# Seven products in place of eight for the first half of the gate's projection, in both layers of a hybrid trunk

## The chip, the cores and the metric

The kernel runs on one core of one Trainium2 chip. The metric is the device time of one execution in microseconds (us), the median of the runs shown. Engines are named as in the profile: PE is TensorE (matmuls), PEld its weight loads, DVE is VectorE, ACT is ScalarE, POOL is GpSimd, SP issues the loads.

## The reference

256 tokens, width 2048, two layers, everything in float32. Cut to what matters here:

```
h = rms_norm(x, norm1_g[l])
q, k, v, gu, gv = split(h @ w_in[l])           # 1024 columns each
attn = dilated_attention(rotary(q), rotary(k), v)        # 8 heads of 128
v2   = layer_norm(gelu(gv)) per group of 128 columns     # gv is "the gate"
gm   = gelu(gu) * (tril(w_spatial) @ v2 + b_spatial)     # 8 groups of 128
x = x + concat(attn, gm) @ w_out[l]
x = x + square(relu(rms_norm(x, norm2_g[l]) @ w_up[l])) @ w_down[l]
out = rms_norm(x, final_g)
```

## The kernel before, in words

Each float32 matmul is made of three in a reduced format: weight and activation are split into a high and a low part, and high·high, low·high and high·low are added in PSUM. The activations `x` lie transposed in SBUF; `hs` holds the two parts of `x` times the norm's gain (the norm's factor itself is multiplied in later).

**Pieces and steps.** The weights come in pieces of 128 x 1024 numbers (`Sub`, L145). SP loads a piece into one of 7 buffers `raw`, ACT copies it into the high part `hi` (L168), DVE subtracts to get the low part `lo` (L178); there are 6 buffers of each, so the sixth piece ahead has to wait until TensorE has left the first. One step of the program uses one piece. There are three kinds:

- a *plain* step (`transposed`, L376): 24 matmuls with 256 columns (L410), the weight is the stationary operand, the result comes out transposed. q and k are made so, in 8 groups of four steps: k0 (256 columns of k), q0, k1, q1, ... q3. After a group come the rotary positions (`after_qk`, L572: two copies on ACT, L577 and L578, then three operations on DVE, L579 to L581);
- a *natural* step (`natural`, L454): 12 matmuls with 512 columns (L470 to L472), 8 steps for 512 columns. v and the gate are made so, in two halves each;
- a *seven-product* step (`fast`, L414), which before is used in the MLP's second matrix alone: Strassen's scheme in Winograd's form on a 2 x 2 block. It has 42 matmuls with 256 columns (L440) and counts as four pieces: `Top` and `Bottom` are loaded, `Sums` twice are made of them by DVE (two subtractions of 128 x 512 each, L219 and L220, L223 and L224), and each of the four needs its `hi` and `lo` (of `Top` half the width). Two such steps make one block of 1024 rows. It also needs sums of the activations, made beforehand by four DVE operations (L803 to L806) and split by `to_half` (L644).

**The order.** Every engine takes its instructions in the order in which the program writes them. The main loop (L1007) goes through the list of steps. For step n it writes, in this order: `hi` of pieces up to five after the step's own (`high_to`; for a `Sums` piece its subtractions as well), what is due (`soon`), `lo` of pieces up to four after (`low_to`), loads, the step's matmuls, what follows a finished group, hooks, and then entries of a queue (`later`) whose delay, counted in pieces, is over. Entries of the list without a piece (`mark`) also let the queue run. So a piece's `lo` is written four pieces ahead, and whatever else DVE and ACT have to do is written between.

**A layer's first half.** v (natural, 16 steps), then k0, q0, k1, q1, ... q3 (32 plain steps), then the gate (natural, 16 steps), the other gate operand gu (plain, 16 steps) and the output matrix. The attention of a pair of heads is put in the queue when its q group ends: `scores` 2 pieces later (TensorE L593, L596; DVE L602, L604), `normalise`, `turn` (transposes), `values`. The gate's halves pass through `gelu`, statistics (`stats`, DVE) and `layer_norm` (POOL).

Of the kernel before, what the change touches and what calls it, by code (L numbers as in the profile page):

```python
# [28 lines left out]
F32 = mybir.dt.float32  # L29
# [38 lines left out]
HALVES = 5  # L68
BEHIND, BETWEEN = 2, 1
D_SCORES, D_NORM, D_TURN, D_VALUES = 2, 1, 3, 2  # L70

# [20 lines left out]
def trunk(ctx: ExitStack, tc: tile.TileContext, layout, xT, consts, gains, w, b_sp, w_sp, out):  # L92
# [8 lines left out]
    pacc = ctx.enter_context(tc.tile_pool(name="pacc", bufs=1, space=bass.MemoryType.PSUM))  # L101
    paux = ctx.enter_context(tc.tile_pool(name="paux", bufs=4, space=bass.MemoryType.PSUM))

# [31 lines left out]
    def acc_bank(i=None, of=4):  # L135
# [277 lines left out]

    def fast(name, l, row0, col0, tiles, slots, fresh, last, done):  # L414

# [5 lines left out]
        for p in range(2):  # L421
# [3 lines left out]
            def mm(p=p, top=top, bottom=bottom, upper=upper, lower=lower):  # L425
                if p == 0:
                    o.extend(slots())
                half = tiles[0][0]
                sums_ready()
                extra = sum_parts[0]  # L430
                left, right = slice(0, 256), slice(256, 512)
# [43 lines left out]
    def mark(fn):  # L475

        steps.append((None, fn, None))

    def from_hs(k):
# [38 lines left out]
    def layer(l, n1, n2, n3, last):  # L518
# [27 lines left out]
        if l:  # L546
            mark(start)
        mix_a, mix_g = [None], [None]
        qk = {}
# [107 lines left out]
        def after_gv(c, ps):  # L657
            z, u = t32("gz", [2, 512], tag="tmpB"), t32("gu", [2, 512], tag="tmpA")
            for tt in range(2):
                act.activation(z[:, tt, :], ps[tt], AF.Copy, scale=n1.half[:, tt:tt + 1])  # L660

            def then(u, z):
# [5 lines left out]
                later(1, 1.5, lambda: stats(c // P))  # L668

            gelu(z, u, then)  # L670

        def stats(g0):
# [8 lines left out]
            later(0, 1.0, lambda: layer_norm(g0))  # L681

        def layer_norm(g0):
            y, mv = par["y"], par["mv"]
            r = t32("lr", [2, 4])
            rsqrt(nc.gpsimd, r, mv[:, :, g0:g0 + 4, 1], 1.0, LN_EPS, [2, 4])
            for g in range(4):
                for tt in range(2):
                    yg = y[:, tt, (g0 + g) * P:(g0 + g + 1) * P]
                    nc.gpsimd.tensor_scalar(yg, yg, mv[:, tt, g0 + g, 0:1], r[:, tt, g:g + 1],  # L690
                                            op0=OP.subtract, op1=OP.mult)
            par["normed"] += 4
# [107 lines left out]
        def sums():  # L800

            a11, a12, a21, a22 = (inner[:, 4 * k:4 * k + 4, t * P:(t + 1) * P] for t in range(2) for k in range(2))
            vec.tensor_tensor(a22, a21, a22, op=OP.add)  # L803
            vec.tensor_tensor(a21, a11, a21, op=OP.subtract)
            vec.tensor_tensor(a11, a22, a11, op=OP.subtract)
            vec.tensor_tensor(a12, a12, a11, op=OP.subtract)  # L806

# [33 lines left out]
        def turn_back(c, first, second, bank):  # L841
# [5 lines left out]
            soon(1, lambda: update(n3, c, ps, False, last))  # L847

        def halves(bank):
            return [bank[:, 0:256], bank[:, 256:512]]  # L850

# [61 lines left out]
        for e in range(9):  # L913
# [5 lines left out]
            if e:  # L919
                w = 512 * len(ORDER.get(e, USUAL))  # L920
                hidden = [hid[e - 1]]
                down = collect(transposed, "w_down", l, (e - 1) * 1024, 8, w, D - w, from_tiles(hidden, NH),
                               lambda c, ps, e=e, w=w: after_down(e, (c + w) // P, ps),
                               apart=last and e == 8, of=2 if e < 8 else 4,
                               cols=None if e < 8 else [c * P for c in LAST])
                for g, at in enumerate(ORDER.get(e, USUAL)):
                    banks = []
                    quick += zip(at, collect(fast, "w_down", l, (e - 1) * 1024, 512 * g, hidden,
                                             (lambda g=g, banks=banks: slots_other(g, banks)) if g else slots_first,
# [146 lines left out]
```

## Time and profile before

| what | before |
|---|---|
| device time, median of 3 runs | 2023.7 us (2023.22 to 2024.14) |
| time of the profiled execution | 2023.7 us, of it 2021.9 us span |
| busy share of the span: PE, DVE, ACT, POOL | 99%, 78%, 60%, 8% |
| granted TensorE clock, mean | 0.997 |
| instructions | 40716, of them 16810 matmuls |

The span is the time from the first to the last instruction on the chip; 1.8 us of the execution lie around it. A line such as L410 is a line of the kernel before.

### The profile page before, as it was taken

Reading aid. Unit: us, or ns where it says so; the run is one execution under the profiler, and the core shown is the slowest. Engines: PE = TensorE matmul, PEld = TensorE weight load, DVE = VectorE, ACT = ScalarE, POOL = GpSimd, SP = SyncE. Lnnn points to the kernel's source line nnn. Section 1 sums busy time; section 2 is a strip of 40 time slices with the busy share of each in tenths; the row PEclk is TensorE's granted clock in tenths of the full one; section 3 lists DMA queues with packets and bytes.
Section 4 is the critical chain, followed back from the end, with each engine's and each line's share of the span. In section 5 each row is a group of like instructions: output and inputs, shape, how many; then the busy total and the mean of one; then the engine's idle time right before and its main releaser. Section 6 shows DMA issues by size and latency. Waiting matters only on the chain.

```text
span 2021.9 us, 40716 instructions
## 1 busy us (share of the span) xinstructions
PE 2009.5 (99%) x16810; PEld 1973.4 (98%) x16810; DVE 1579.8 (78%) x1954; ACT 1221.2 (60%) x1613; POOL 156.2 (8%) x200
## 2 busy tenths in 40 slices
PE   9999999999999999999999999999999999999997
PEld 8998999999999999999989989999999999999997
DVE  7566766688888898898856667667888898888985
ACT  7565455566566666665645654556666666667653
POOL 0002300000001000100000032000000000010000
PEclk9999999999999999999999999999999999999998
DMA  9555556566678776866664555565676776777662
GB/s 330 192 167 167 187 189 202 174 229 204 222 219 239 240 225 203 249 215 215 201 215 158 168 187 188 188 199 179 217 229 208 228 236 216 239 220 241 212 215 81
DMA packets 126442, 419.26 MB, mean 207 GB/s; under 512 B 14128, under 2 KB 22064, under 8 KB 126256
## 3 DMA queue, kind: packets, MB, share of 16 engines
q1 hardware_dynamic: 110800, 389.86, 57.2%
q0 software_dynamic: 14304, 23.86, 6.5%
q8 instruction: 131, 2.15, 0.4%
q10 hardware_dynamic: 1152, 2.94, 0.4%
q14 instruction: 55, 0.45, 0.1%
HBM read 394.58 MB, written 22.02 MB: 206 GB/s over the span
## 4 chain that ended last, share of the span: by engine, by line
PE 99%; DVE 0%; ACT 0%; issue 0%; DVEq 0%
PE acc L410 70%; PE acc L440 10%; PE aux L440 8%; PE acc L470 3%; PE acc L472 3%; PE acc L471 3%; PE aux L699 0%; PE aux L635 0%; PE aux L593 0%; PE aux L622 0%; PE aux L994 0%; DVE x L1038 0%; PE aux L596 0%; PE aux L637 0%; PE acc L846 0%; PE aux L539 0%
## 5 line engine op out<-in xcount | busy, mean ns | idle before, releaser
L168 ACT ACTIVATE hi<-raw 128x1024 fp32r<-128x1024 f32 (+1 forms) x817 | 836.9, 1050 | 487.5 <-DVE raw L220 216.2
L178 DVE TENSOR_TENSOR lo<-raw,hi 128x1024 fp32r<-128x1024 f32 (+1 forms) x817 | 965.3, 1214 | 143.4 <-ACT hi L168 140.4
L410 PE MATMUL acc<-hs,hi 128*128 128x256 f32 x5632 | 985.9, 277 | 0.0
L410 PEld LDWEIGHTS acc<-hs,hi 128*128 128x128 f32 x5632 | 857.9, 188 | 0.4 <-issue 0.2
L410 PE MATMUL acc<-hs,lo 128*128 128x256 f32 x2816 | 778.0, 276 | 0.0
L410 PEld LDWEIGHTS acc<-hs,lo 128*128 128x128 f32 x2816 | 528.7, 188 | 0.4 <-issue 0.2
L410 PE MATMUL acc<-half,hi 128*128 128x256 f32 x2688 | 462.2, 276 | 0.0
L410 PEld LDWEIGHTS acc<-half,hi 128*128 128x128 f32 x2688 | 406.7, 188 | 0.0
L410 PE MATMUL acc<-half,lo 128*128 128x256 f32 x1344 | 371.0, 276 | 0.0
L410 PEld LDWEIGHTS acc<-half,lo 128*128 128x128 f32 x1344 | 252.3, 188 | 0.0
L873 POOL DMA_DIRECT2D far<-ar x92 | 74.2, 816 | 1164.4 <-ACT ar L876 563.9
L440 PE MATMUL acc<-hi,shared 128*128 128x256 f32 x768 | 138.4, 276 | 0.0
L440 PEld LDWEIGHTS acc<-hi,shared 128*128 128x128 f32 x768 | 119.2, 188 | 0.0
L440 PE MATMUL aux<-hi,half 128*128 128x256 f32 x528 | 110.6, 276 | 0.0
L440 PE MATMUL acc<-lo,shared 128*128 128x256 f32 x384 | 106.0, 276 | 0.0
L649 DVE TENSOR_TENSOR half<-ar,half 128x512 fp32r<-128x512 f32 x72 | 49.8, 691 | 68.6 <-ACT half L646 68.6
L470 PE MATMUL acc<-hi,hs 128*128 128x512 f32 x256 | 101.8, 398 | 0.0
L472 PE MATMUL acc<-hi,hs 128*128 128x512 f32 x256 | 100.6, 393 | 0.0
L471 PE MATMUL acc<-lo,hs 128*128 128x512 f32 x256 | 100.3, 392 | 0.0
L440 PEld LDWEIGHTS aux<-hi,half 128*128 128x128 f32 x528 | 87.2, 188 | 0.0
L440 PE MATMUL aux<-hi,shared 128*128 128x256 f32 x448 | 80.7, 276 | 0.0
L510 DVE TENSOR_TENSOR x<-x,acc 128x512 f32<-128x512 f32 (+1 forms) x49 | 33.1, 675 | 59.1 <-PE acc L410 57.3
(150 smaller groups left out, 1955.3 us busy)
## 6 DMA issues: line engine op xcount, KB each, us to landing
raw<-in_w SPq DMA_DIRECT2D x731, 512.0 KB, 4.7
far<-ar POOLq DMA_DIRECT2D x60, 256.0 KB, 8.3
far<-ar POOLq DMA_DIRECT2D x32, 128.0 KB, 4.3
ar<-far POOLq DMA_DIRECT2D x12, 256.0 KB, 9.7
raw<-in_w SPq DMA_DIRECT2D x10, 256.0 KB, 5.1
x<-in_xT SPq DMA_DIRECT2D x7, 256.0 KB, 5.9
out<-x SPq DMA_DIRECT2D x7, 256.0 KB, 3.1
shared<-in_b_sp ACTq DMA_DIRECT2D x2, 512.0 KB, 7.7
```

The lines of the kernel that those rows point to most:

```text
L168: act.activation(self.h[:, j * m:(j + 1) * m], self.raw[:, j * m:(j + 1) * m], AF.Copy)
L178: vec.tensor_tensor(lo[:, r], self.raw[:, r], self.h[:, r].bitcast(F32), op=OP.subtract)
L410: pe.matmul(o, lhsT=lhs, rhs=xs[:, rhs, :], start=(first and j == 0), stop=(last and j == 2), skip_group_check=True)
L440: calls.append(lambda k=k, j=j, lhs=lhs, rhs=rhs: pe.matmul(o[n], lhsT=lhs, rhs=rhs, start=(p == 0 and k == 0 and j == 0 and n in fresh), ...
L470: pe.matmul(ps, lhsT=xh, rhs=hi, start=(k0 + k == 0), stop=False)
L471: pe.matmul(ps, lhsT=xh, rhs=lo, start=False, stop=False)
L472: pe.matmul(ps, lhsT=xl, rhs=hi, start=False, stop=(k0 + k == KC - 1))
L510: vec.tensor_tensor(xj, xj, ps[j][:, 0:S] if alone else pair(ps)[:, j, :], op=OP.add)
L649: vec.tensor_tensor(t[:, c:c + 2, 1, :], src, t[:, c:c + 2, 0, :].bitcast(F32), op=OP.subtract)
L873: nc.gpsimd.dma_start(far[g][:, r], src, **({} if e == max(g, 1) else {"accum_op": OP.add}))
```

## The change

In both layers the first 512 columns of the gate no longer are eight natural steps behind q3. They become four seven-product steps, two for each half of the 2048 rows, put into the list of q and k steps ahead of the places 3, 6 (rows 0 to 1023) and 16, 24 (rows 1024 to 2047). Their seven results stand in four PSUM banks until they are added up (`gather`) when five pieces have passed since the last of them; the gate's first half then waits in SBUF and goes through `gelu` while the second half is made in natural steps. The sums of activations for the first half of the rows are made during the last steps of v, those for the second half ahead of place 4 (`seven_sums`: eight ACT copies, four DVE operations) and places 9 to 12 (`seven_parts`). The first half's layer norm is done on DVE in place of POOL; the last pair of heads is transposed one piece sooner. While four auxiliary banks are short, one tile of the scores uses an accumulator bank. The diff without its repetitions:

```
+SEVEN, AGAIN = ((3, 6), (16, 24)), 8
 D_SCORES, D_NORM, D_TURN, D_VALUES = 2, 1, 3, 2
...
+    aux_at, aux_held = [3], set()
     def aux_bank():
-        return paux.tile([P, 512], F32, name="aux", tag="aux")
+        i = next(j % 4 for j in range(aux_at[0] + 1, aux_at[0] + 5) if j % 4 not in aux_held)
+        aux_at[0] = i
+        return paux.tile([P, 512], F32, name=f"aux{i}", tag=f"aux{i}")
...
+    def strassen_sums(f, i, n):
+        a11, a12, a21, a22 = (f[:, 4 * k + i:4 * k + i + n, t * P:(t + 1) * P] for t in range(2) for k in range(2))
+        vec.tensor_tensor(a22, a21, a22, op=OP.add)
+        vec.tensor_tensor(a21, a11, a21, op=OP.subtract)
+        vec.tensor_tensor(a11, a22, a11, op=OP.subtract)
+        vec.tensor_tensor(a12, a12, a11, op=OP.subtract)
...
-            s1, s0 = aux_bank(), aux_bank()
+            s1, s0 = aux_bank(), acc_bank(1 - bank_at[0]) if aux_held else aux_bank()
...
-            later(D_TURN, 0.5, lambda: turn(j, p1, p0))
+            later(D_TURN - (j == 3), 0.5, lambda: turn(j, p1, p0))
...
+        def seven_slots():
+            if "o" not in seven:
+                banks = [acc_bank(2), acc_bank(3)]
+                for _ in range(2):
+                    banks.append(aux_bank())
+                    seven.setdefault("aux", []).append(aux_at[0])
+                aux_held.update(seven["aux"])
+                seven["o"] = [h for b in banks for h in halves(b)][0:7]
+            return seven["o"]
...
+        def seven_sums(rows):
...
+            f = seven["plain"][rows]
+            for k in range(NH):
+                c = NH * rows + k
+                act.activation(f[:, k, :], x[:, c, :], AF.Copy, scale=g_all[:, n1.g, c:c + 1])
+            strassen_sums(f, 0, 4)
+        def seven_parts(rows, k):
+            to_half(seven["sums"], k, seven["plain"][rows][:, k:k + 2, :])
+        def seven_done(o):
+            soon(5, lambda: gather(o))
+        def gather(o):
+            z = t32("gz", [2, 512], tag="tmpB")
+            p1, p2, p3, p5, p7, p6, p4 = o
+            c11, c12, c21, c22 = (z[:, tt, h * S:(h + 1) * S] for tt in range(2) for h in range(2))
+            act.activation(c12, p1, AF.Copy)
+            vec.tensor_tensor(c11, c12, p2, op=OP.add)
...
+            aux_held.clear()
+            seven["z"] = z
...
-            rsqrt(nc.gpsimd, r, mv[:, :, g0:g0 + 4, 1], 1.0, LN_EPS, [2, 4])
+            e = nc.gpsimd if g0 else vec
+            rsqrt(e, r, mv[:, :, g0:g0 + 4, 1], 1.0, LN_EPS, [2, 4])
...
+        hook(base + 13, lambda: seven_sums(0))
+        for k in range(0, NH, 2):
+            hook(base + 14 + k // 2, lambda k=k: seven_parts(0, k))
+        plain = []
         for j in range(4):
-            transposed("w_in", l, 0, KC, AW + j * 256, 256, from_hs, lambda c, ps, j=j: after_qk("k", j, ps))
-            transposed("w_in", l, 0, KC, j * 256, 256, from_hs, lambda c, ps, j=j: after_qk("q", j, ps))
-        natural("w_in", l, 4 * AW, AW, after_gv)
+            for name, col in (("k", AW), ("q", 0)):
+                plain += collect(transposed, "w_in", l, 0, KC, col + j * 256, 256, from_hs,
+                                 lambda c, ps, j=j, name=name: after_qk(name, j, ps), of=2)
+        quick = {}
+        for rows in range(2):
+            quick.update(zip(SEVEN[rows], collect(fast, "w_in", l, 1024 * rows, 4 * AW, seven_forms(rows), seven_slots,
+                                                  () if rows else (0, 2, 4, 6), range(7) if rows else (),
+                                                  seven_done if rows else None)))
...
+        for i, one in enumerate(plain):
+            if quick.get(i):
+                steps.append(quick[i])
+            if i == 4:
+                mark(lambda: seven_sums(1))
+            if AGAIN < i <= AGAIN + 4:
+                mark(lambda k=2 * (i - AGAIN - 1): seven_parts(1, k))
+            steps.append(one)
+        late = collect(natural, "w_in", l, 4 * AW + 512, 512, lambda c, ps: soon(1, lambda: after_gv(512, ps)))
+        for i, one in enumerate(late):
+            if i == 5:
+                mark(lambda: gate_half(0, seven["z"]))
+            steps.append(one)
```

Three places of the order of instructions. First DVE behind the rotary positions of k0, in the first layer. Before, the four `lo` of the next plain steps follow and then the positions of q0:

```order
L579 TENSOR_TENSOR ar_80<-acc1_565,cosR_553 128x512
L580 TENSOR_TENSOR ar_80<-ar_80,sinR_554 128x512
L581 TENSOR_TENSOR ar_80<-ar_80 128x512
L178 TENSOR_TENSOR lo_699<-raw_512,hi_662 128x1024
L178 TENSOR_TENSOR lo_730<-raw_514,hi_697 128x1024
L178 TENSOR_TENSOR lo_760<-raw_532,hi_728 128x1024
```

Now (L594 to L596 are the positions, L485 to L488 the sums of activations, `plain` their tile, L183 is `lo`, L224 to L229 are the subtractions of the second seven-product step's weights):

```order
L224 TENSOR_TENSOR raw_526<-raw_526 128x2x256
L225 TENSOR_TENSOR raw_526<-raw_528,raw_526 128x2x256
L228 TENSOR_TENSOR raw_528<-raw_528,raw_526 128x2x256
L229 TENSOR_TENSOR raw_528<-raw_528 128x2x256
L594 TENSOR_TENSOR ar_80<-acc1_583,cosR_567 128x512
L595 TENSOR_TENSOR ar_80<-ar_80,sinR_568 128x512
L596 TENSOR_TENSOR ar_80<-ar_80 128x512
L485 TENSOR_TENSOR plain_502<-plain_502 128x4x128
L486 TENSOR_TENSOR plain_502<-plain_502 128x4x128
L487 TENSOR_TENSOR plain_502<-plain_502 128x4x128
L488 TENSOR_TENSOR plain_502<-plain_502 128x4x128
L183 TENSOR_TENSOR lo_803<-raw_526,hi_750 128x1024
```

`lo_803`, of the third piece of the step at place 6, stands behind the positions and the four sums; the 20th matmul of that step is the first that reads it.

Second, ACT at the same place. Before, around the two copies for the positions of k0:

```order
L168 ACTIVATE hi_632<-raw_488 128x1024
L168 ACTIVATE hi_662<-raw_512 128x1024
L577 ACTIVATE ar_80<-acc1_565 64x512
L578 ACTIVATE ar_80<-acc1_565 64x512
L168 ACTIVATE hi_697<-raw_514 128x1024
```

Now (`hi_750` and `hi_801` are the third and the fourth piece of the step at place 6, L717 are the eight copies from which the sums are made):

```order
L191 ACTIVATE hi_736<-raw_526 128x512
L173 ACTIVATE hi_738<-raw_528 128x1024
L173 ACTIVATE hi_750<-raw_526 128x1024
L592 ACTIVATE ar_80<-acc1_583 64x512
L593 ACTIVATE ar_80<-acc1_583 64x512
L717 ACTIVATE plain_502<-x_84,cols_82 128x256 x8
L173 ACTIVATE hi_801<-raw_528 128x1024
```

The two copies now follow `hi_750`, which needs two of the subtractions, and the eight copies follow them.

Third, DVE between the positions of q0 and the first scores. Before, two `lo` stand there, of one plain step each:

```order
L580 TENSOR_TENSOR ar_80<-ar_80,sinR_554 128x512
L581 TENSOR_TENSOR ar_80<-ar_80 128x512
L178 TENSOR_TENSOR lo_825<-raw_594,hi_788 128x1024
L178 TENSOR_TENSOR lo_856<-raw_636,hi_823 128x1024
L602 SCALAR_TENSOR_TENSOR ar_80<-aux_884,con_81 128x512
```

Now one `lo` and the first of the second sums' low parts (L664):

```order
L595 TENSOR_TENSOR ar_80<-ar_80,sinR_568 128x512
L596 TENSOR_TENSOR ar_80<-ar_80 128x512
L183 TENSOR_TENSOR lo_995<-raw_836,hi_958 128x1024
L664 TENSOR_TENSOR half_503<-plain_502,half_503 128x2x256
L617 SCALAR_TENSOR_TENSOR ar_80<-aux3_1026,con_81 128x512
```

The mark ahead of place 9 lets the queue run before that step, so the scores stand behind one plain step of k1 and no longer behind two.

## Rows read from the trace of the kernel before

**Rows 1.** The page: the span, and the first engine's busy time and share.
```profile
span 2021.9 us, 40716 instructions
...
PE 2009.5 (99%) x16810; PEld 1973.4 (98%) x16810; DVE 1579.8 (78%) x1954; ACT 1221.2 (60%) x1613; POOL 156.2 (8%) x200
```

**Rows 2.** Waits of PE, whole run: us in total, times, longest.
```profile
PE aux L328 <- DVE nr L354: 1.2, 1, 1.2
PE aux L994 <- DVE warm L990: 1.1, 1, 1.1
```

**Rows 3.** Chain that ended last, second layer's first half: start, us, what.
```profile
1053.84 27.22 PE acc L410 x240
1081.06 0.86 PE aux L593 x4
...
1176.52 0.24 PE acc L470
...
1198.51 13.62 PE acc L410 x120
```

**Rows 4.** The same chain in the first layer's MLP.
```profile
408.75 4.54 PE aux L440 x40
```

**Rows 5.** Stretch of q, k and gate, second layer: busy us by engine, clock, DMA.
```profile
1053.84:1198.50 144.66, 144.66 (x1050) 135.84 (x1050) 86.85 (x115) 82.12 (x131) 9.82 (x18) 1.00 0.53 175
```

**Rows 6.** Groups by line and shape: count, busy us, mean ns, idle before.
```profile
L178 DVE TENSOR_TENSOR lo<-raw,hi 128x1024 fp32r<-128x1024 f32 x807 | 958.7, 1220 | 139.3 <-ACT hi L168 136.2
...
L191 DVE TENSOR_TENSOR lo<-raw,hi 128x512 fp32r<-128x512 f32 x76 | 52.0, 684 | 2.1 <-ACT hi L186 2.1
...
L649 DVE TENSOR_TENSOR half<-ar,half 128x512 fp32r<-128x512 f32 x72 | 49.8, 691 | 68.6 <-ACT half L646 68.6
```

**Rows 7.** Timeline of DVE behind k0, second layer: start, us, what.
```profile
1066.02 0.69 DVE L579 TENSOR_TENSOR ar<-acc,cosR 128x512 f32<-128x512 f32 x1 [4.37 <-ACT ar L578]
...
1067.95 4.62 DVE L178 TENSOR_TENSOR lo<-raw,hi 128x1024 fp32r<-128x1024 f32 x4
```

**Rows 8.** Timeline of ACT behind k0, second layer.
```profile
1064.77 0.60 ACT L577 ACTIVATE ar<-acc 64x512 f32<-64x512 f32 x1 [1.66 <-PE acc L410]
```

**Rows 9.** Timeline of DVE in the MLP, around weight sums and activation sums.
```profile
1425.27 0.68 DVE L219 TENSOR_TENSOR raw<-raw 128x512 f32<-128x512 f32 x1
...
1428.05 4.77 DVE L178 TENSOR_TENSOR lo<-raw,hi 128x1024 fp32r<-128x1024 f32 x4
...
1442.61 0.69 DVE L803 TENSOR_TENSOR ar<-ar 128x512 f32<-128x512 f32 x1
...
1445.40 1.22 DVE L178 TENSOR_TENSOR lo<-raw,hi 128x1024 fp32r<-128x1024 f32 x1
```

**Rows 10.** Timeline of ACT in the MLP, behind two weight sums.
```profile
1426.78 1.06 ACT L168 ACTIVATE hi<-raw 128x1024 fp32r<-128x1024 f32 x1 [2.83 <-DVE raw L220]
```

**Rows 11.** Timeline of ACT at the start: copies with a gain.
```profile
17.45 0.89 ACT L287 ACTIVATE hs<-x,cols 128x256 fp32r<-128x256 f32 x2
```

**Rows 12.** Chain that ended last, first layer's first half.
```profile
1.06 5.06 PE aux L994 x22
6.12 0.46 PE acc L470
...
57.07 1.72 PE aux L539 x4
```

**Rows 13.** Timeline of DVE, first layer, behind those four matmuls.
```profile
57.97 2.16 DVE L543 SCALAR_TENSOR_TENSOR shared<-aux,cols,shared 128x128 f32<-128x128 f32 x8 [2.67 <-PE aux L539]
```

**Rows 14.** Three stretches at the end: length, busy us of PE first, clock third last.
```profile
2007.80:2009.45 1.65, 1.61 (x15) 1.52 (x14) 0.39 (x1) 1.22 (x4) 0.00 (x0) 1.00 0.00 0
2009.45:2010.62 1.17, 0.01 (x1) 0.01 (x1) 0.71 (x5) 0.26 (x1) 0.00 (x0) 1.00 0.00 0
2010.62:2011.80 1.18, 1.17 (x4) 0.87 (x4) 0.00 (x0) 0.00 (x0) 0.00 (x0) 0.54 0.00 0
```

**Rows 15.** Timeline of POOL, second layer's second layer norm.
```profile
1217.29 10.71 POOL L690 TENSOR_SCALAR shared<-shared,mv,lr 128x128 f32<-128x128 f32 x8
```

More of the change, by code (lines that the diff above doesn't have):

```diff
@@ L101, in trunk @@
     pacc = ctx.enter_context(tc.tile_pool(name="pacc", bufs=1, space=bass.MemoryType.PSUM))
-    paux = ctx.enter_context(tc.tile_pool(name="paux", bufs=4, space=bass.MemoryType.PSUM))
+    paux = ctx.enter_context(tc.tile_pool(name="paux", bufs=1, space=bass.MemoryType.PSUM))
     vec, act, pe = nc.vector, nc.scalar, nc.tensor
@@ L412, in transposed, with fast @@
             steps.append((wt, mm, (lambda c=c: after(c, accs[c])) if k0 + 4 == nk else None))
-    def fast(name, l, row0, col0, tiles, slots, fresh, last, done):
+    def fast(name, l, row0, col0, forms, slots, fresh, last, done):
         o = []
@@ L427, in mm @@
                     o.extend(slots())
-                half = tiles[0][0]
-                sums_ready()
-                extra = sum_parts[0]
+                half, extra = forms()
                 left, right = slice(0, 256), slice(256, 512)
@@ L477, in mark, with halves @@
         steps.append((None, fn, None))
+    def strassen_sums(f, i, n):
[4 more added lines that the diff above has]
+        vec.tensor_tensor(a12, a12, a11, op=OP.subtract)
+    def halves(bank):
+        return [bank[:, 0:256], bank[:, 256:512]]
     def from_hs(k):
@@ L547, in layer @@
             mark(start)
+            mark(lambda: bank_at.__setitem__(0, 2))
         mix_a, mix_g = [None], [None]
@@ L657, in after_gv, with gate_half @@
         def after_gv(c, ps):
-            z, u = t32("gz", [2, 512], tag="tmpB"), t32("gu", [2, 512], tag="tmpA")
+            z = t32("gz", [2, 512], tag="tmpB")
             for tt in range(2):
                 act.activation(z[:, tt, :], ps[tt], AF.Copy, scale=n1.half[:, tt:tt + 1])
+            gate_half(c, z)
+        def gate_half(c, z):
+            u = t32("gu", [2, 512], tag="tmpA")
             def then(u, z):
@@ L667, in then @@
                 vec.scalar_tensor_tensor(par["y"][:, :, c:c + 512], u, 1.0, z, op0=OP.add, op1=OP.mult)
-                later(1, 1.5, lambda: stats(c // P))
+                if c:
+                    later(1, 1.5, lambda: stats(c // P))
+                else:
+                    stats(0)
             gelu(z, u, then)
+        seven = {}
+        def seven_slots():
[7 more added lines that the diff above has]
+            return seven["o"]
@@ new lines, in seven_forms @@
+        def seven_forms(rows):
+            return lambda: (hs[:, NH * rows:NH * (rows + 1)], seven["sums"])
+        def seven_sums(rows):
+            if "sums" not in seven:
+                f = tp.tile([P, 2, NH, S], F32, name="plain", tag="half", bufs=2)
+                seven["plain"] = [f[:, i, :, :] for i in range(2)]
+                seven["sums"] = tp.tile([P, NH, 2, S], F32R, name="half", tag="half", bufs=2)
+            f = seven["plain"][rows]
[3 more added lines that the diff above has]
+            strassen_sums(f, 0, 4)
@@ new lines, in seven_parts @@
+        def seven_parts(rows, k):
[3 more added lines that the diff above has]
+        def gather(o):
+            z = t32("gz", [2, 512], tag="tmpB")
+            p1, p2, p3, p5, p7, p6, p4 = o
+            c11, c12, c21, c22 = (z[:, tt, h * S:(h + 1) * S] for tt in range(2) for h in range(2))
+            act.activation(c12, p1, AF.Copy)
+            vec.tensor_tensor(c11, c12, p2, op=OP.add)
+            vec.tensor_tensor(c12, c12, p6, op=OP.add)
+            vec.tensor_tensor(c22, c12, p7, op=OP.add)
+            vec.tensor_tensor(c12, c12, p5, op=OP.add)
+            vec.tensor_tensor(c21, c22, p4, op=OP.subtract)
+            vec.tensor_tensor(c12, c12, p3, op=OP.add)
+            vec.tensor_tensor(c22, c22, p5, op=OP.add)
+            for tt in range(2):
+                act.activation(z[:, tt, :], z[:, tt, :], AF.Copy, scale=n1.half[:, tt:tt + 1])
+            aux_held.clear()
+            seven["z"] = z
@@ L680, in stats @@
                     vec.bn_aggr(mv[:, tt, g0 + g, :], st[:, tt, g, :])
-            later(0, 1.0, lambda: layer_norm(g0))
+            if g0:
+                later(0, 1.0, lambda: layer_norm(g0))
+            else:
+                soon(1, lambda: layer_norm(0))
         def layer_norm(g0):
@@ L689, in layer_norm @@
                     yg = y[:, tt, (g0 + g) * P:(g0 + g + 1) * P]
-                    nc.gpsimd.tensor_scalar(yg, yg, mv[:, tt, g0 + g, 0:1], r[:, tt, g:g + 1],
-                                            op0=OP.subtract, op1=OP.mult)
+                    e.tensor_scalar(yg, yg, mv[:, tt, g0 + g, 0:1], r[:, tt, g:g + 1],
+                                    op0=OP.subtract, op1=OP.mult)
             par["normed"] += 4
@@ L800, in sums @@
         def sums():
[L802 to L806, printed above, removed]
+            strassen_sums(inner, 0, 4)
             def parts(k):
@@ L847, in turn_back @@
             soon(1, lambda: update(n3, c, ps, False, last))
-        def halves(bank):
-            return [bank[:, 0:256], bank[:, 256:512]]
         held = []
@@ L921, in layer, with forms @@
                 hidden = [hid[e - 1]]
+                def forms(tile=hid[e - 1]):
+                    sums_ready()
+                    return tile[0], sum_parts[0]
                 down = collect(transposed, "w_down", l, (e - 1) * 1024, 8, w, D - w, from_tiles(hidden, NH),
```

4 lines of the change are left out of this document (3 added, 1 removed).

## The prediction

> **What bounds the kernel now.** I read the page first: TensorE is busy 99% of a span of 2021.9 us [rows 1]. Next its waits: two, of 1.2 and 1.1 us, one at each end of the run [rows 2]. So between them TensorE never stands still, and the time is the number of matmuls times their spacing. The chain of waits gives the spacing, since its pieces follow each other without a hole. Ten plain steps, 240 matmuls of 256 columns, take 27.22 us: 0.1134 each and 2.72 a step [rows 3]. The gate's second half, 96 matmuls of 512 columns, runs from 1176.52 to 1198.51: 21.99 us for eight natural steps [rows 3]. In a seven-product step 40 matmuls take 4.54, so 42 take 4.77 [rows 4]. Last the stretch of q, k and gate by engine: in 144.7 us VectorE (DVE) works 86.9 and ScalarE (ACT) 82.1, both with room [rows 5]. The question is whether the room lies where the new work falls.
>
> **The matmuls.** Per layer eight natural steps go (-21.99) and four seven-product steps come (4 x 4.77 = +19.07): -2.92, and -5.84 in both layers. The weights stay eight loaded pieces, so the load traffic is the same. The sum below is made against the profiled execution, whose 2023.7 us (2021.9 of span and 1.8 around it) equal the median.
>
> **The step at place 6, second layer.** Let T be the time from k0's first matmul. Six plain and one seven-product step lie ahead of place 6 (the places at 3 and 6 are not far apart): it begins at 6 x 2.72 + 4.77 = 21.1, and its 20th matmul, the first to read the low part of its third piece, is due at 21.1 + 19 x 0.1134 = 23.3. When does DVE have that part? Its work before it begins with the first activation sums. ACT makes the eight copies for them after the third-last step of v begins (T = -8.2, three natural steps of 2.75) and after one `hi` (1.06): a pair of such copies takes 0.89 with 0.50 for a single one [rows 11], so eight take 7 x 0.40 + 0.50 = 3.3, and DVE can start at -3.9. From there to the low part asked for, in program order:
> - twice four activation sums, 2.79 each time (1442.61 to 1445.40) [rows 9]: 5.6
> - eight weight subtractions, four in 2.78 (1425.27 to 1428.05) [rows 9]: 5.6
> - nine full `lo`, 1.15 each back to back (4.62 for four) [rows 7], and two of half width, 0.68 [rows 6]: 11.7
> - four low parts of sums at 0.69 [rows 6]: 2.8
> - the rotary positions of k0, 1.93 (1066.02 to 1067.95) [rows 7].
>
> That is 27.6 us, so without any pause the part would be there at 23.7, already 0.4 late. Three pauses come on top, since DVE and ACT wait for each other in turn. (1) The second part of the sums stands on ACT behind a `hi` and two copies of v: 1.1. (2) The third piece's `hi` starts only when two of the subtractions are done (0.1 after the second in the MLP [rows 10]) and takes 1.06; the positions' two copies stand behind it in ACT's order, so k0's positions wait 0.9 after the last subtraction, though k0 ended long before. (3) The eight copies for the second sums follow there (3.3), and DVE, done with the positions, waits another 1.3. Sum 3.3: the part is there at 27.0, and TensorE waits 27.0 - 23.3 and 0.1 for the signal, **3.8 us**.
>
> Bounds: at best ACT is free when k0 ends (four plain and one seven-product step, T = 15.7). From there the positions' copies take 1.25 (1064.77 to 1066.02 [rows 7, 8]), the eight copies 3.3, the sums 2.79, the `lo` 1.22: 8.6 us where TensorE takes 23.3 - 15.7 = 7.6. So at least **1.0**. At worst every instruction costs its full mean (1.22 a `lo` [rows 6]), 0.7 more: **4.5**. I take 3.8, since DVE's count alone already fills the time.
>
> **The same, first layer.** DVE has one more `lo` behind the first sums (1.15), the tables of the positions (about 0.8) and eight operations of the spatial shift (2.16 [rows 13]) in between; TensorE has the shift's four matmuls (1.72 [rows 12]) and four small ones (0.45), so its 20th matmul is due at 25.4. The sums begin at -4.3; 27.6 + 4.1 of work and 2.0 of pauses end at 29.3: **3.9**, with the bounds of above.
>
> **Scores of the first heads.** They stood two plain steps (5.4) behind q0, now one (2.72). The positions need 3.2 from the end of the group (1064.77 to 1067.95 for k0 [rows 7, 8]), so TensorE waits about 0.5 in each layer, 1.1 with signals. Bounds 0.8 and 1.6. The scores of the other heads keep 5.4 or more.
>
> **What I cost at nothing.** At place 3 the last low part comes, by the same walk, 0.5 before its matmul; behind places 16 and 24 the positions of q1 and q2 (3.2) and one `lo` (1.2) end at 4.5, and the plain step that reads it starts at 4.8. These are thin covers: if each is missed by 0.3 to 0.5 in both layers, 2 to 3 us. `gather` (seven DVE operations of half of 128 x 512) stands where four `lo` are already ahead, 10.9 us of TensorE; uncovered it costs under 3 us a layer. The first layer norm on DVE, some twelve short operations and eight of about 0.27 (as in [rows 13]), has the same cover. The second half's norm on POOL starts some 8 us later than before, counted from the end of the gate; it ended at 1228.0, 29.5 us after that end [rows 3, 15], and its first matmuls come about 37 us after it and need half of it. The score tile in an accumulator bank is read by DVE more than a step before the bank is wanted.
>
> **Sum.** -5.84 + 3.8 + 3.9 + 1.1 = +3.0: **2026.7 us**. By 0.2% or 4.05 us, about what a measurement of this kernel tells from no change, that is the same: its bounds on that side are 2019.7 and 2027.7.
>
> **The rivals.**
>
> *The whole gain* (2023.7 - 5.84 = **2017.9**). For it: 58 of 145 us of DVE are free in the stretch, and the MLP has such steps in plenty with no wait of TensorE [rows 2, 5]. Against it: there DVE's room is ahead of the step, here it is behind, and the chain from k0's end is too long even with idle engines. Only if copies and sums were much faster than their rows would this come. 8%.
>
> *Smaller waits*: only the chain from k0's end counts, 1.0 in each layer, and 1.1 for the scores: -5.84 + 3.1, **2021.0**. Against it speaks the count of 27.6 us, for it that some pauses may overlap. 15%.
>
> *The clock falls* (slower). At the end of the run the dense matmuls stop at 2007.7, short ones of one column follow to 2009.4, and the granted clock goes from 1.00 to about half around 2010.7, 1.2 us into the idle time and some 3 us after the dense work [rows 14]. A wait of 3.8 in the middle is longer. If it falls there, the matmuls behind run at half the level until it rises; at the start TensorE had been at work from 1.06 to about 7.0 before a natural matmul's spacing fell from 0.46 to 0.23 [rows 12], 5.9 us at half the level, which loses 3.0. Decisive point: whether the granted clock leaves 1.00 in or right behind the wait at place 6. Once: **2029.6**, in both layers: **2032.6**. Against it: no wait of this length follows dense matmuls of full width in this trace, and the one that does is not of one kind. 32%. The Trainium skill ("TensorE: Matmul & The Clock Gate", section "HAM oscillation — how this bites in real kernels") warns of the same thing: idle gaps between bursts of matmuls let the array fall to its lower clock, so that the next burst starts slow. The trace agrees in its last stretch; that it happens in a wait like this one no row shows.
>
> *The thin covers fail*: places 3, 16 and 24 each wait 0.5 in both layers, +3: **2029.7**. 7%.
>
> **How the numbers follow.** My forecast, waits of 2.8 to 4.5 at place 6 and no fall of the clock, has 38% and its own range 2024.7 to 2028.1; some 15% of it lies above 2027.7. Faster by over 0.2%: 0.08. Slower: 32 + 7 + 6 = 0.45. The same: 15 + 32 = 0.47. The range 2021.0 to 2031.5 leaves out the whole gain, a part of the smaller waits and the clock falling for its full length in both layers.
>
> **What would show it.** The waits of TensorE list a line for the seven-product matmuls ending on a `lo` of DVE, two times and about 3.8 us each, and one for the first scores ending on the positions, two of about 0.5. DVE then shows the four activation sums starting some 7 us after k0's end, released by ACT's copies. The natural lines shrink from 256 to 192 matmuls each. The granted clock in the 6 us behind the wait tells the third rival: 1.00 or near half. The forecast is wrong if the seven-product step at place 6 runs through as those of the MLP do, or if TensorE waits at a place that I cost at nothing.

## The result and the profile after

The changed kernel takes 2030.32 us in the median (2029.82 to 2031.86) against 2023.35 (2023.16 to 2024.14) for the kernel before beside it: ratio 1.0035, 95% interval 1.0026 to 1.0045. It is slower, by 7 us or 0.35%. The profiled execution is 2029.82, or 6.1 above that of before.

The page of the changed kernel (span, first line of engines), the answer to [rows 1]:

```profile
span 2028.0 us, 41160 instructions
...
PE 2008.2 (99%) x16954; PEld 1979.1 (98%) x16954; DVE 1645.7 (81%) x2084; ACT 1250.9 (62%) x1679; POOL 129.5 (6%) x158
```

TensorE's share still rounds to 99%, so the page does not show where the loss is. Its waits (us in total, times, longest) do, beside the two lines of [rows 2]:

```profile
PE acc L443 <- DVE lo L183: 6.3, 2, 3.3
PE aux L608 <- DVE ar L596: 1.2, 2, 0.6
PE aux L333 <- DVE nr L359: 1.2, 1, 1.2
PE aux L1091 <- DVE warm L1087: 1.1, 1, 1.1
```

Two of these lines are new: seven-product matmuls wait for a `lo` of VectorE, once a layer, and the first scores for the rotated q0. (A third new one, of 0.2 us, stands at the start of the run.) The wait of 3.00 us in the second layer, seen on VectorE (start, us, what, idle before), beside [rows 7, 9]:

```profile
1057.80 1.29 DVE L664 TENSOR_TENSOR half<-plain,half 128x512 fp32r<-128x512 f32 x2 [0.31 <-ACT half L661]
...
1063.21 0.69 DVE L664 TENSOR_TENSOR half<-plain,half 128x512 fp32r<-128x512 f32 x1 [0.19 <-ACT half L661]
...
1073.40 0.69 DVE L229 TENSOR_TENSOR raw<-raw 128x512 f32<-128x512 f32 x1
1075.08 0.69 DVE L594 TENSOR_TENSOR ar<-acc,cosR 128x512 f32<-128x512 f32 x1 [0.98 <-ACT ar L593]
...
1078.41 0.69 DVE L485 TENSOR_TENSOR plain<-plain 128x512 f32<-128x512 f32 x1 [1.32 <-ACT plain L717]
...
1081.20 2.35 DVE L183 TENSOR_TENSOR lo<-raw,hi 128x1024 fp32r<-128x1024 f32 x2
```

The first two rows are the pause ahead of the second part of the first sums (1.1 in the prediction, 0.31 + 0.19 here). The pauses of 0.98 and 1.32 are the other two that the prediction named (0.9 and 1.3): VectorE stands behind the positions' copies and then behind the eight copies for the second sums. Now the granted clock round that wait, which the matmul at 1082.47 ends (length, busy us of PE first, clock third last), where [rows 5] had 1.00 throughout:

```profile
1079.50:1082.50 3.00, 0.03 (x1) 0.03 (x1) 2.93 (x5) 3.00 (x4) 0.00 (x0) 1.00 0.00 0
1082.50:1083.00 0.50, 0.50 (x4) 0.50 (x5) 0.50 (x1) 0.50 (x1) 0.00 (x0) 1.00 0.00 0
1083.00:1084.00 1.00, 1.00 (x9) 1.00 (x9) 1.00 (x2) 0.11 (x1) 0.00 (x0) 0.78 0.44 98
1084.00:1085.00 1.00, 1.00 (x7) 1.00 (x7) 1.00 (x2) 0.59 (x1) 0.00 (x0) 0.50 1.00 393
1085.00:1086.00 1.00, 1.00 (x6) 1.00 (x6) 1.00 (x2) 0.46 (x1) 0.00 (x0) 0.50 0.74 188
1086.00:1087.00 1.00, 1.00 (x7) 1.00 (x6) 1.00 (x2) 0.00 (x0) 0.00 (x0) 0.52 0.89 262
1087.00:1088.00 1.00, 1.00 (x11) 1.00 (x11) 1.00 (x1) 0.87 (x1) 0.00 (x0) 1.00 0.98 291
```

The clock holds through the wait, falls to the lower level (1.2 of 2.4 GHz) about 1 us after TensorE has resumed, and is back at 1087. Lost: 0.22 + 0.50 + 0.50 + 0.48 = 1.70 us. The first layer shows the same behind its wait of 3.30 us, 0.7 us after TensorE has resumed. Last the chain of the second layer, beside [rows 3]:

```profile
1127.36 11.31 PE acc L415 x96
1139.32 8.48 PE acc L415 x72
1147.80 2.83 PE acc L443 x24
1158.21 11.31 PE acc L415 x96
1170.17 8.48 PE acc L415 x72
```

The same groups take 10.90, 8.18 and 2.72 in the first layer. At granted clock 1.00 a matmul here takes 0.1178 us in place of 0.1135. Before, that spacing held in one group a layer, between the first scores and their transposes (11.31 for 96 matmuls, from 81.88 and from 1082.37). In the changed kernel's second layer it begins at a pause of 0.05 us behind the step at place 16, where a matmul comes 0.16 us behind the last in place of 0.11:

```profile
1121.82 0.33 PE L415 MATMUL acc<-hs,lo 128*128 128x256 f32 x1
1121.98 0.40 PE L415 MATMUL acc<-hs,hi 128*128 128x256 f32 x2
```

**The account of the 6.1 us**: matmuls -5.84; waits at place 6 +6.3; scores +1.2; clock 2 x 1.70 = +3.4; the slower spacing 1.53 from the five rows, less 2 x 0.41 of before: +0.7. Sum +5.8; 0.3 stays unassigned. That 0.3 is itself made of unlike parts: q and k begin 0.6 earlier than before (50.80 against 51.37), and what follows the gate in the second layer takes 0.7 less (822.7 against 823.4 us), so that some 1.6 in the two stretches stands in no term. Part of it is slower spacing outside the five rows and pauses too short to be listed.

### The profile page after: what moved, and what is told of

Same layout as the page of the kernel before. It is cut to its first block, busy times and chain, and to the rows that moved or that the text cites. A ratio compares the mean times of both kernels' runs of the same rounds, so it can differ in the third digit from the quotient of the medians.

```text
span 2028.0 us, 41160 instructions
## 1 busy us (share of the span) xinstructions
PE 2008.2 (99%) x16954; PEld 1979.1 (98%) x16954; DVE 1645.7 (81%) x2084; ACT 1250.9 (62%) x1679; POOL 129.5 (6%) x158
## 4 chain that ended last, share of the span: by engine, by line
PE 98%; DVE 1%; DMA 0%; ACT 0%; issue 0%; ACTq 0%; DVEq 0%
PE acc L415 70%; PE acc L443 11%; PE aux L443 9%; PE acc L473 2%; PE acc L475 2%; PE acc L474 2%; PE aux L608 0%; PE aux L774 0%; PE aux L650 0%; PE aux L637 0%; DVE x L1135 0%; DMA cols<-in_gains 0%; PE aux L652 0%; PE acc L941 0%; PE aux L553 0%
## 5 line engine op out<-in xcount | busy, mean ns | idle before, releaser
L183 DVE TENSOR_TENSOR lo<-raw,hi 128x1024 fp32r<-128x1024 f32 (+1 forms) x825 | 973.9, 1213 | 123.7 <-ACT hi L173 120.5
L443 PE MATMUL aux<-hi,half 128*128 128x256 f32 x592 | 124.9, 280 | 0.0
L664 DVE TENSOR_TENSOR half<-ar,half 128x512 fp32r<-128x512 f32 x72 | 49.8, 691 | 64.7 <-ACT half L661 64.7
L443 PEld LDWEIGHTS aux<-hi,half 128*128 128x128 f32 x592 | 99.0, 191 | 0.0
L443 PE MATMUL acc<-hi,half 128*128 128x256 f32 x448 | 85.6, 276 | 0.0
L443 PE MATMUL aux<-lo,half 128*128 128x256 f32 x296 | 82.8, 280 | 0.0
L473 PE MATMUL acc<-hi,hs 128*128 128x512 f32 x192 | 76.6, 399 | 0.2 <-ACT hs L292 0.2
```

The costliest lines, as they stand in the source:

```text
L183: vec.tensor_tensor(lo[:, r], self.raw[:, r], self.h[:, r].bitcast(F32), op=OP.subtract)
L443: calls.append(lambda k=k, j=j, lhs=lhs, rhs=rhs: pe.matmul(o[n], lhsT=lhs, rhs=rhs, start=(p == 0 and k == 0 and j == 0 and n in fresh), ...
L473: pe.matmul(ps, lhsT=xh, rhs=hi, start=(k0 + k == 0), stop=False)
L664: vec.tensor_tensor(t[:, c:c + 2, 1, :], src, t[:, c:c + 2, 0, :].bitcast(F32), op=OP.subtract)
```

## The experiments

The theory after the result: the order of work on VectorE and ScalarE makes the wait, TensorE's pause makes the clock fall, and the pauses, not the seven products, are what costs. The rival: 27.6 us of VectorE work in front of the step are too many, wherever it stands. Ratios are against the kernel before, on the same chip.

**1. The step at place 8** (e1)

```diff
-SEVEN, AGAIN = ((3, 6), (16, 24)), 8
+SEVEN, AGAIN = ((3, 8), (16, 24)), 8
```

> The second step of the first pair stands at place 8 in place of place 6; nothing else differs. Theory (the wait is made by the order of work on VectorE and ScalarE behind the second activation sums, and the clock falls because TensorE paused): two more natural steps lie between the sums and the step, some 22 us, so the 3.3 and 3.0 us waits go, the half-speed stretch behind them (about 3.4 us, some 1.7 us lost) goes in both layers, and the waits before the scores (0.6 us each) go too, since a seven-product step now stands between: 2030.3 - 6.3 - 3.3 - 1.2 = 2019.5, between 2018.5 and 2021.5. Rival (VectorE's added work, 27.6 us of sums, costs the time wherever it stands): within 1 us of 2030.3.

Measured: 2025.86 (2025.04 to 2029.01), ratio 1.0014 [1.0005, 1.0023]. The two steps that now lie between are plain ones, 2 x 2.72 = 5.4 us, and not natural ones of 22 as the expectation has it. The step itself and the scores no longer wait (0.16 us left), but the plain step right behind it does. TensorE in the second layer:

```profile
1087.78 0.28 PE L443 MATMUL aux<-hi,hs 128*128 128x256 f32 x1
1090.46 0.39 PE L415 MATMUL acc<-hs,lo 128*128 128x256 f32 x1 [2.41 <-DVE lo L183]
```

The wait was moved on by one step and became 0.6 to 1.0 shorter. Theory and rival are both half right: it is the backlog of VectorE's queue that waits, wherever it is first needed.

**2. The second sums later** (e2)

```diff
-            if i == 4:
+            if i == 8:
                 mark(lambda: seven_sums(1))
```

> The step stays at place 6; the second activation sums (eight ScalarE copies and the VectorE sums that follow) are started four marks later, behind that step's own work. Theory: the copies no longer stand ahead of the step's third piece, which VectorE can then split by about 1078.3 us against 1079.3 due, so the wait and the clock's fall go; the 0.6 us before the scores stay: 2030.3 - 6.3 - 3.3 = 2020.7, between 2019.5 and 2022.5, unless the sums now come late for the steps at place 16, which would show as a wait there. Rival (VectorE's load and not its order): same amount of work, so within 1 us of 2030.3.

Measured: 2029.73, ratio 1.0031 [1.0019, 1.0042]. No wait at place 6, as the theory has it; instead two a layer at place 16 and behind it, second layer:

```profile
1116.88 0.38 PE L443 MATMUL acc<-lo,half 128*128 128x256 f32 x1 [1.05 <-DVE lo L183]
1122.52 0.38 PE L415 MATMUL acc<-hs,lo 128*128 128x256 f32 x1 [2.43 <-DVE lo L183]
```

The theory's number fails, the rival's holds: put off, the same work is late at the next seven-product pair.

**3. The pause filled** (e3): 26 matmuls that nobody reads, in TensorE's wait.

```diff
+                    if spare and p == 1 and at == 19:
+                        for _ in range(26):
+                            pe.matmul(spare(), lhsT=hs[:, 0, 0, 0:P], rhs=hs[:, 0, 0, :], start=False, stop=False,
+                                      skip_group_check=True)
                     call()
```

> 26 matmuls whose result nothing reads (128x256, into the half bank that the seven products leave free) stand ahead of the 20th matmul of the step at place 6, in both layers: 26 x 0.1135 = 2.95 us of TensorE work where it waited 3.3 and 3.0 us. VectorE and ScalarE do the same work as before at the same times. Theory (the clock fell because TensorE paused): lateness of the third piece is unchanged, so no pause to be won, but the granted clock stays 1.00 and the half-speed loss goes: 2030.3 - 3.3 = 2027.0, between 2026.3 and 2027.8. Rival (the clock falls for another reason, such as this stretch's kind of matmul): clock falls as before, 2030.3, or up to 2031 if the added matmuls run on into the due time.

Measured: 2028.93 in the median, ratio 1.0026 [1.0015, 1.0037], above the theory's range; the profiled run took 2026.55 where the theory had 2027.0. In that run the third piece is as late as before (the added matmuls and 0.21 us of wait stand where 3.30 were), and the clock behind it, first layer, stays up:

```profile
80.00:81.00 1.00, 0.79 (x6) 0.68 (x6) 1.00 (x2) 0.96 (x2) 0.00 (x0) 1.00 0.00 0
81.00:82.00 1.00, 1.00 (x11) 1.00 (x10) 1.00 (x2) 0.03 (x1) 0.00 (x0) 1.00 0.75 225
82.00:84.00 2.00, 2.00 (x19) 2.00 (x19) 2.00 (x3) 1.44 (x2) 0.00 (x0) 1.00 0.77 272
```

Clock 1.00 in both layers with the same kind of matmul behind: the pause is the cause. The seven runs agree, with mean clocks of 0.997 and 0.998 where the changed kernel's six have 0.995 and 0.996. But they spread from 2026.08 to 2031.13, the three slowest at 0.998, so something else costs up to 5 us.

**4. The copies early** (e4): only ScalarE's eight copies for the second sums stand ahead of q and k.

```diff
...
+            if k == (4 if l else 2):
+                hook(base + 14 + k // 2, lambda: seven_copies(1))
```

> Of the second activation sums only the eight ScalarE copies are made earlier, ahead of the first step of q and k; the VectorE sums start at the same place of the order as before. Theory: the wait shrinks by the time that the sums stood waiting for the copies (1.32 us of VectorE's idle time ahead of them): 1.7 to 2.0 us left in each layer. If a wait of that length still makes the clock fall: 2030.3 - 2.6 = 2027.7; if not: 2024.4. Rival (the wait is VectorE's count of work alone): wait and time as before, 2030.3 within 0.7.

Measured: 2025.86 (2022.64 to 2028.56), ratio 1.0011 [1.0002, 1.0020]; waits 1.90, as foretold, and 1.59, a little below it. In the profiled run, the fastest, the clock holds behind both. Its spread asked for a second trace, of the same kernel:

> The kernel with the copies early a second time, for its trace: its runs spread from 2022.6 to 2028.6 us while the kernel before stays within 0.8 us of its median, and the profiled one was the fastest. Theory (the matmuls' spacing takes one of two values after a pause, 0.1135 or 0.118 us, and keeps it for tens of us): a slower run shows the same waits within 0.2 us, granted clock 1.00, and stretches at 0.118. Rival (a wait of 1.9 us sometimes makes the clock fall and sometimes not): a slower run shows granted clock 0.50 behind a wait, some 1.7 us for each.

Measured: 2024.89, with waits of 1.90 and 1.58 at the same places. First layer, the first trace and then the second, from the end of the wait on:

```profile
78.20:79.00 0.80, 0.71 (x6) 0.71 (x7) 0.80 (x2) 0.00 (x0) 0.00 (x0) 1.00 0.00 0
79.00:80.00 1.00, 1.00 (x11) 1.00 (x10) 1.00 (x2) 0.06 (x1) 0.00 (x0) 1.00 0.60 172
```

```profile
78.80:79.50 0.70, 0.62 (x4) 0.62 (x5) 0.70 (x2) 0.00 (x0) 0.00 (x0) 0.75 0.00 0
79.50:80.00 0.50, 0.50 (x4) 0.50 (x4) 0.50 (x2) 0.00 (x0) 0.00 (x0) 0.50 0.28 82
80.00:81.00 1.00, 1.00 (x7) 1.00 (x7) 1.00 (x1) 0.00 (x0) 0.00 (x0) 0.50 0.85 270
```

Here the rival wins: the same wait lets the clock fall in one run and not in another, 1.7 of the 2.25 us between them. Another 0.6 is the start of the run: q and k begin at 51.72 against 51.12.

**5. The second sums ahead of q and k** (e5), copies and VectorE's part together, the step at place 6.

```diff
+        hook(base + 12, lambda: seven_sums(1))
         hook(base + 13, lambda: seven_sums(0))
...
-            if i == 4:
-                mark(lambda: seven_sums(1))
```

> The second activation sums, copies and VectorE sums together, are made ahead of q and k, in front of the first ones; the step stays at place 6. Theory (VectorE's queue is what is late: what counts is how much work stands ahead of the third piece's split and how long VectorE idled before it): in layer 2 VectorE idled 4.67 us ahead of the first sums, which now takes up the 2.9 us, so no wait at place 6; in layer 1 it idled 1.6 us there and 1.2 us later, so of the wait, 1.90 us when only the copies came early, about 0.7 us stays, or stands at place 3 instead. Waits 0.7 + 1.0 (scores) on 2023.4 - 5.8: 2019.3 where the matmuls keep 0.1135 us, up to 2.3 us a layer more where they run at 0.118: 2019 to 2023. Rival (only the place in the order at place 6 matters, as first thought): no waits but the scores' in either layer, 2018.6. Other rival (the earlier work makes the last steps ahead of q and k late): a new wait of up to 2.9 us ahead of place 3, 2022 or more.

Measured: 2024.04 (2022.03 to 2025.57), ratio 1.0001 [0.9992, 1.0010]. No wait at place 6 in either layer; in the first layer 1.42 us at place 3. The theory's place was the second of its two and its size (0.7) too small. The time lies above its range of 2019 to 2023; in the profiled run, the slowest, matmuls at 0.118 us cost some 2.5 us in each layer.

**6. The scores one step later**, on top of the early copies (e7)

```diff
-D_SCORES, D_NORM, D_TURN, D_VALUES = 2, 1, 3, 2
+D_SCORES, D_NORM, D_TURN, D_VALUES = 3, 1, 3, 2
```

> Copies early as in the kernel before this one of that kind (2025.86 us, waits of 1.90 and 1.59 us at place 6, 0.51 us twice ahead of the scores), and the scores one step later in all eight places. Theory: the scores' wait goes and nothing else moves: 1.0 us less in waits, 2024.8 in the median and 2021.6 in the fastest run. Rival (scores start the chain of softmax, transposes and values, and one step later each collides with the next q): new waits ahead of the transposes or the last values, no gain or up to 1 us of loss.

Measured: 2026.05, ratio 1.0014 [1.0005, 1.0023], no gain. The scores' wait is gone, but the plain steps behind place 16 now wait 0.95 and 1.24:

```profile
PE acc L443 <- DVE lo L183: 3.5, 2, 1.9
PE acc L415 <- DVE lo L183: 2.2, 2, 1.2
```

That is the rival's loss, at another place than it named.

**7. Both: place 8, sums ahead** (e8), the edits of 1 and 5 together, studied twice.

> The second step of the first pair at place 8 and the second activation sums ahead of q and k, both changes together. Theory (VectorE's queue): the step at place 8 has 4.3 us more of natural steps in front and the sums are out of the way, so neither the 2.3 us wait behind the step at place 8 nor one at place 6, nor the scores' wait: no wait over 0.3 us in the two stretches, clock 1.00 there, 2023.4 - 5.8 = 2017.6, and 2017 to 2020 with stretches at the slower spacing. Rival (VectorE's added work costs the time wherever it stands): waits of some 2 us a layer somewhere, 2021.5 to 2026.

> The kernel with the step at place 8 and the sums ahead a second time: it was 2021.28 us in the median, but the profiled run, 2023.27, was its slowest, with matmuls at 0.118 us in layer 1 from 116 to 172 us behind a wait of 0.15 us. Theory (the spacing is chosen anew at each pause or change of work and differs from run to run): a run of about 2021 us shows the same waits within 0.1 us, granted clock 1.00 in both stretches, and some 2 us less of matmuls at 0.118. Rival (the 2 us were a wait or the clock): the waits differ. Faster than the kernel before once more, ratio 0.998 to 0.9995.

Measured: 2021.28 (2020.77 to 2023.27), ratio 0.9990 [0.9981, 0.9998], and 2022.67 (2020.65 to 2024.83), ratio 0.9996 [0.9987, 1.0005]: clear of the kernel before in the first study alone, and short of the theory's 2017.6. One wait of 1.42 us is left, in the first layer at place 3, where the theory had none over 0.3; the clock stays at 1.00. The second trace has the same waits, and its first layer has no slow groups from 116 to 172 us, where the first trace had nothing else: so the spacing does differ between runs of one program. (Its q and k begin 1.9 us later, at 53.22 against 51.29, which takes back most of that gain.) It does not differ freely, though. In both traces the second layer has a short pause inside the step at place 3 (no wait is printed for it), here in the second:

```profile
1064.78 0.39 PE L443 MATMUL acc<-hi,half 128*128 128x256 f32 x2
1065.17 0.39 PE L443 MATMUL acc<-lo,half 128*128 128x256 f32 x1
```

Two matmuls should take 0.23, and the third starts after 0.39. From there to the first scores everything runs at 0.118.

**8. In the first layer only the copies ahead** (e9); second layer as in 7.

```diff
+        hook(base + 12, lambda: seven_copies(1))
+        if l:
+            hook(base + 12, lambda: seven_sums(1))
...
-            if i == 4:
+            if i == 4 and not l:
                 mark(lambda: seven_sums(1))
```

> As the kernel with both changes, but in layer 1 only the copies stand ahead of q and k and VectorE's second sums come behind the step at place 3, as in the changed kernel; layer 2 as it was. Theory (VectorE's queue): the 1.42 us wait at place 3 of layer 1 goes, since 2.9 us of VectorE's work leave its way; the wait behind the step at place 8 comes back, 2.32 us when the copies came late, less the 1.3 us that VectorE then idled for them: about 1.0. Sum -0.4: 2020.9 beside 2021.3, between 2020 and 2022.5. Rival (a step at place 8 with early copies has no wait at all): 2019.9.

Measured: 2021.16 (2019.79 to 2024.75), ratio 0.9992 [0.9983, 1.0001]. The wait left place 3 and stands behind place 8 instead, 1.43 for 1.42, where about 1.0 was expected: moved, not shortened.

**9. The sums two and four steps earlier** than in 7 (e10, e11)

```diff
-        hook(base + 12, lambda: seven_sums(1))
+        hook(base + 10, lambda: seven_sums(1))
```

(8 in the second kernel.)

> The kernel with both changes (step at place 8, second sums ahead of q and k; 2021.28 and 2022.67 us in its two studies), the second sums two steps earlier still. There layer 1 waited 1.42 us at place 3, and in layer 2 a pause of some 0.2 us inside the step at place 3 was followed by 24 us of matmuls at 0.118 us (about 1 us lost), which the kernel with the copies alone ahead had neither of. Theory (VectorE's queue makes the pauses, and the slower spacing begins at a pause, however short): VectorE's 1.5 us of idle time in front of the norm's factor in layer 1 and 4.8 us in front of the sums in layer 2 take up the 2.9 us, so neither pause is left, and layer 2 keeps 0.1135 from the step at place 3 to the first scores: about 2019.5, between 2018 and 2021.5. Rival (the spacing is independent of the pause): pauses gone, 0.118 us there as before, 2020.5. Rival (the sums now hold up the last steps ahead of q and k in layer 1): a new wait there of 1 to 3 us, 2022 to 2024.

> The same four steps earlier rather than two. Theory: VectorE's queue in layer 1 is no shorter at any place from here on, so as the kernel with two steps, 2019.5, between 2018 and 2021.5. Rival (the eight copies on ScalarE, 3.3 us, now stand ahead of the splits of the first steps, whose weights are only just loaded in layer 1): a wait ahead of q and k in layer 1 of 1 to 3 us, 2021 to 2023.

Measured, two steps: **2018.51** (2017.76 to 2019.31), ratio **0.9974** [0.9965, 0.9984], the version that beats both kernels by the most, and with the least spread of the variants. Of the waits for `lo` in the stretch 2 x 0.15 us are left. The chain behind the step at place 3 of the second layer, in the second trace of experiment 7 and then here:

```profile
1068.28 14.02 PE acc L415 x119
1082.29 2.82 PE acc L443 x24
```

```profile
1065.07 13.50 PE acc L415 x119
1078.56 2.72 PE acc L443 x24
```

With the pause the spacing of 0.118 is gone, as the theory has it. Where a pause too short to be listed stays, so does the spacing: first layer of the same run, a matmul that comes 0.16 us behind the last, and what follows:

```profile
64.98 0.33 PE L443 MATMUL aux<-lo,half 128*128 128x256 f32 x1
65.14 0.40 PE L443 MATMUL aux<-hi,half 128*128 128x256 f32 x2
```

```profile
66.59 14.02 PE acc L415 x119
```

Four steps earlier: 2022.08, ratio 0.9991 [0.9982, 1.0000]. The rival's time and place come out: TensorE waits at v, at the lower clock behind it:

```profile
39.30 0.61 PE L474 MATMUL acc<-lo,hs 128*128 128x512 f32 x1 [2.01 <-DVE lo L183]
39.71 0.63 PE L475 MATMUL acc<-hi,hs 128*128 128x512 f32 x1
```

Its reason, ScalarE's copies, is not what TensorE waited for. The matmul before, at 36.90, reads that step's `hi` and ran in time; the `lo` (38.03 to 39.25) was late, behind the four sums on VectorE. One of these took 2.80 us where the others take 0.69, beside an operation of POOL:

```profile
33.48 2.63 POOL L545 TENSOR_TENSOR shared<-shared,con 128x1024 f32<-128x1024 f32 x1 [33.03 <-DMA raw<-in_w]
```

```profile
33.86 2.80 DVE L486 TENSOR_TENSOR plain<-plain 128x512 f32<-128x512 f32 x1
36.69 0.69 DVE L487 TENSOR_TENSOR plain<-plain 128x512 f32<-128x512 f32 x1
```

Without these 2.1 us the `lo` would have ended at 37.1, just ahead of its matmul at 37.3. With the sums two steps earlier it is a `lo` that runs beside the same operation of POOL (3.44 us in place of 1.22) and TensorE does not wait there; that POOL causes it was not tried.

## Why the prediction came out as it did

The forecast was 2026.7, with 2024.7 to 2028.1 for its own case. The measured 2030.32 lies above that; it lies in the whole range, 2021.0 to 2031.5, because the range took in the third rival.

- **The matmuls, -5.84**: right. In the best version the profiled run is 5.14 under that of before. Its own slow groups cost some 1.1 more than at 0.1135 (the 14.02 above for 13.50, 2.83 for 2.72 behind it, and one group of 8.48 for 8.18 in the second layer are most of it), before has 0.82 of such, and two short pauses add 0.3: -5.84 + 1.1 - 0.82 + 0.3 = -5.3.
- **The wait at place 6, 3.8 and 3.9**: mechanism right, size a little high, 3.00 and 3.30. The pauses of 0.98 and 1.32 are as counted, and taking the third away shortened the waits by 1.40 and 1.41 where 1.3 was counted. What was sized too high in the second layer is above all the first pause: 1.1 counted, 0.31 + 0.19 in the rows.
- **The scores, 1.1**: right, 1.2.
- **The covers costed at nothing** held in the changed kernel: no listed wait at places 3, 16 and 24, and behind 16 the pause of 0.05. They were as thin as said. The sums put in front of place 3, or the scores moved beside place 16, turned them into waits of 1.42 and of 0.95 to 1.24.
- **The step that failed is the clock**: the likeliest case kept it at 1.00. The third rival happened, in both layers, and at 1.70 us a fall rather than the 3.0 read from [rows 12]: the start's half-speed stretch was longer than the one behind a wait. With 1.70 that rival comes to 2026.7 + 3.4 = 2030.1; measured 2029.82. That the two are so near is partly luck, since waits sized 1.4 too high stand against the terms that nobody counted. [Rows 14] was the right row to weigh: there the lower clock came some 3 us after the dense work, and the waits here are of 3.00 and 3.30. Experiment 3 shows that the pause is the cause. The Trainium skill ("TensorE: Matmul & The Clock Gate", section "HAM oscillation — how this bites in real kernels") says that idle gaps make the next burst start slow; the trace agrees on the burst, though its first 0.7 and 1.1 us in the changed kernel still ran at 1.00.
- **Not foreseen**: the spacing of 0.118, +0.7 in the profiled run. It stood in the trace of before, in the groups behind the first scores, and was passed over there, as the sum took every matmul at 0.1134. Half of the 1.4 by which the waits were sized too high is cancelled by it.

What the wait comes from has two halves. The order decides where the backlog is met (experiments 1, 2 and 8 only moved it); what takes it away is starting the sums where VectorE was idle anyway: two steps earlier its work falls into the 1.5 us ahead of the norm's factor and the 4.8 us ahead of the first sums (experiment 9). Why a pause leaves one spacing or the other stays open.

## What to carry to other kernels

When TensorE never waits, price a new wait at more than its length: here 3 us of waiting cost another 1.7 of lower clock, and behind some pauses of 0.05 to 0.2 us, though not behind all, the matmuls ran slower and lost some 0.8 to 1.7 us each time. A wait made by a full queue moves when a step or its work is shifted, and goes only when the work is placed where that queue idles. Walk the queue's work against each due time on all places, not only at the one that is latest, and look for the point where moving it earlier holds up what comes before.

## What the runs showed that was not expected

- **What the clock did behind each wait over 1.4 us in the stretches of q, k and gate**: behind 3.30 and 3.00 it fell; behind 2.43, 2.43, 2.41 and 2.32 (experiments 1, 2) in two of four; behind 1.90, 1.90 and 1.89 (the early copies' three traces) in two of three; behind 1.59, 1.58 and 1.59, and behind four of 1.42 or 1.43, never. Each of the six falls cost 1.7 us. Between 1.89 and 2.43 us the length does not decide: in one trace (experiment 1) the clock fell behind 2.32 and held behind 2.41.
- **Two spacings at granted clock 1.00**: 0.1135 or 0.118 us for 128 x 256. In the fourteen traces here, the changes from one to the other came at a pause (of 0.05 us and more) or at other matmuls in between (scores, transposes). A pause does not always bring the slow one: the same wait of 1.42 us in experiment 7 was followed by 0.118 in one run and by 0.1135 in the other. With the falls of the clock and the start of the run (q and k begin between 50.80 and 53.22 us in the traces without a wait of 2 us ahead of them) this is probably what spreads the runs of some variants over 4 to 6 us, where those of before stay within 2; that was not tried by itself.
